# Transfers by index that name 128 rows instead of 96, in a mixture-of-experts kernel on one core

## The chip, the cores and the metric

The kernel runs on one core of one Trainium2 chip. The metric is the device time of one execution in microseconds (us). Before the change the median of three runs was 1855.05 us (1853.5 to 1856.7).

## What is computed

Two layers work on 512 latent tokens and 256 context tokens of width 1024. Each layer is a token mixer (retention and pooling) and then a mixture of 32 SwiGLU experts. The router gives each token two experts, and each expert computes on the tokens that it was given:

```python
def run_block(args):
    tok, e = args
    xb = h_pad[tok]
    return (jax.nn.silu(xb @ w_gate[e]) * (xb @ w_up[e])) @ w_down[e]
...
y_buf = y_buf.reshape(n_rows, D).astype(jnp.float32) * buf_w[:, None]
return jax.ops.segment_sum(y_buf, buf_tok, num_segments=T + 1)[:T].astype(h.dtype)
```

The first layer routes all 768 tokens, the second the 512 latent tokens alone. Weights are float32, and every expert has three matrices of 2 MiB each, so that each expert's weights are 6 MiB that are read once.

## The kernel before

The program is written out by hand for each engine, in order, with no scheduler; the names PE (TensorE), DVE (VectorE), ACT (ScalarE), POOL (GpSimd) and SP (the queue that issues the weight loads) are those of the profile.

Weights. `pump()` (L141) issues loads of 1 MiB each on SP into a ring of seven `raw` tiles; six loads make an expert. ACT (L1335) turns a `raw` tile into a float16 high part, DVE (L1340) makes the low part that is left, and the `raw` tile is then free for the next load. One of the six (the second half of the down matrix) is kept as float32 and is read by PE itself (L1283).

Tokens. Each expert has a capacity of CAP = 96 slots, numbered from 0 without holes; an expert with more tokens would go to `overflow_blocks` (L1347), which none does for these inputs. `rt.si[slot, e]` is the token's row, and for a slot without a token it is a number past the last row (8192 is added in L1106 and L1107). `fetch` (L1212) is a DMA by index: it reads the rows of 4 KB that the 96 slots of an expert name from `hs` in HBM into `xg`, slot by slot, and skips a row whose index is out of bounds. The slots with a token are called live below, the others dead. `turn` (L1219) transposes `xg` on PE, and `turned` (L1230) copies the result for the matmuls, the second half of it on ACT (L1234).

Results. `down_out` (L1286, ACT) writes the weighted result of an expert into a tile `ye` of 128 x 2 x 1024 float32, of which rows 0 to 95 are used; in the first layer `gate_rows` (L1289, POOL) fills the second half of that tile with the gate of each row. `scatter` (L1298) multiplies by the gate on POOL (L1303), and `scatter_rows` (L1306) is again a DMA by index: it adds the 96 rows of 4 KB to the rows of `xs` in HBM that the index names, and skips those out of bounds.

Order. In the loop over experts (L1539), expert e's down projection and scatter are followed by the transposition of expert e+2's rows and by the fetch for expert e+4, then by expert e+1's up projection. POOL therefore sees, per expert: gate rows, two multiplications, a scatter, a fetch. The tiles `whi`, `wlo`, `wd`, `ye`, `xg` and some others share a pool `G` of 14 buffers, and a new tile takes a free one.

Of the kernel before, what the change touches and what calls it, by code (L numbers as in the profile page):

```python
# [8 lines left out]
F32 = mybir.dt.float32  # L9
# [9 lines left out]
D = 1024  # L19
# [7 lines left out]
CAP = 96  # L27
# [14 lines left out]
def kernel(ctx: ExitStack, tc: tile.TileContext, a: dict, out: bass.AP):  # L42
# [10 lines left out]
    def G(shape, dt, name):  # L53
        return pg.tile(shape, dt, name=name, tag="G")
# [4 lines left out]
    def W(shape, dt, name="wt"):  # L59
        return pw.tile(shape, dt, name=name, tag="W")  # L60

    def S(shape, dt=F32, name="st"):
        return ps_.tile(shape, dt, name=name, tag="S")

    def P(shape, name="pt"):
        return pp.tile(shape, F32, name=name, tag="P")

    V, A, Q, T = nc.vector, nc.scalar, nc.gpsimd, nc.tensor
# [5 lines left out]
    hs = [pd.tile([(6 - 2 * l) * 128, 2 * D], F16, name=f"hs{l}") for l in range(DEPTH)]  # L74
# [98 lines left out]
    for j in range(2):  # L173
        t = G([128, 2, D], F32, "x")
# [856 lines left out]
    class Route:  # L1031


        def __init__(self, l, nt):
            self.nt = nt
            self.tmp = G([128, nt, 232], F32, "rtmp")
            self.L = self.tmp[:, :, 0:40]
            V.memset(self.L[:, :, 36:40], -1e30)
            self.ix = W([128, nt, 16], U32, "rix")
            self.oh = W([128, nt, 32], F16, "roh")  # L1040
            self.v4 = pc.tile([128, nt, 32, 4], F16, name=f"rv{l}", tag="rv")
            self.posm = pc.tile([128, nt, 32], F32, name=f"rp{l}", tag="rp")
            self.ov = pc.tile([128, 6, 32], F32, name=f"ov{l}", tag="ov")

            self.si = pc.tile([128, 32], I32, name=f"si{l}", tag="si")
            self.sv = pc.tile([128, 2, 32], F32, name=f"sv{l}", tag="sv")
            self.novi = pc.tile([1, 1], I32, name=f"nov{l}")

        def choose(self, i, between=()):
# [162 lines left out]
    def fetch(l, xg, si):  # L1212

        Q.indirect_dma_start(  # L1214
            out=xg[0:CAP], out_offset=None, in_=hs[l],
            in_offset=bass.IndirectOffsetOnAxis(ap=si, axis=0), bounds_check=(6 - 2 * l) * 128 - 1,
            oob_is_err=False)

    def turn(xg):  # L1219

        out = []
        for r in range(2):
            pt = pp.tile([128, KC, CAP], F16, name="pgx", tag="P")
            for c in range(KC):
                o = r * D + c * 128
                T.transpose(pt[:, c, :], xg[0:CAP, o:o + 128], ident16[0:CAP, 0:CAP])
            out.append(pt)
        return out

    def turned(pts):  # L1230
        xh = W([128, KC, CAP], F16, "xh")
        xl = W([128, KC, CAP], F16, "xl")
        V.tensor_copy(xh, pts[0])  # L1233
        A.copy(xl, pts[1])  # L1234
        return xh, xl

    def slot_vals(pe, v4e, nt):
        pv = P([128, 512], "psv")
        for i in range(nt):
            T.matmul(pv[0:CAP, 0:4], lhsT=pe[:, i, :], rhs=v4e(i), start=(i == 0), stop=(i == nt - 1))  # L1240
        sv = S([128, 8], F32, "sv")
        si = S([128, 1], I32, "si")
        V.tensor_copy(sv[0:CAP, 0:1], pv[0:CAP, 0:1])
        V.tensor_reduce(sv[0:CAP, 1:2], pv[0:CAP, 1:4], axis=AX.X, op=ALU.add)
        V.tensor_scalar(sv[0:CAP, 1:2], sv[0:CAP, 1:2], IWS / VS, None, op0=ALU.mult)
        V.tensor_scalar(sv[0:CAP, 2:3], sv[0:CAP, 0:1], 0.5, 8192.0, op0=ALU.is_lt, op1=ALU.mult)
        V.scalar_tensor_tensor(si[0:CAP], sv[0:CAP, 0:1], -1.0, sv[0:CAP, 2:3], op0=ALU.add, op1=ALU.add)
        V.tensor_scalar(sv[0:CAP, 3:4], sv[0:CAP, 0:1], NLAT + 0.5, None, op0=ALU.is_gt)
        return sv, si
# [39 lines left out]
    def gate_rows(yg, ctx, g2r, nv):  # L1289

        if nv == 1:
            return [g2r[0:CAP, 0, n * 512:(n + 1) * 512] for n in range(2)]
        gn = yg[0:CAP, 1, :]
        Q.tensor_scalar(gn, g2r[0:CAP, 1, :], ctx, None, op0=ALU.mult)  # L1294
        Q.tensor_tensor(gn, gn, g2r[0:CAP, 0, :], op=ALU.add)
        return [gn[:, n * 512:(n + 1) * 512] for n in range(2)]

    def scatter(l, yg, si, gs, eng):  # L1298

        yt = yg[:, 0, :]  # L1300
        for n in range(2):
            yn = yt[0:CAP, n * 512:(n + 1) * 512]
            eng.tensor_tensor(yn, yn, gs[n], op=ALU.mult)  # L1303
        scatter_rows(l, yg, si)

    def scatter_rows(l, yg, si):  # L1306
        Q.indirect_dma_start(  # L1307
            out=xs[l], out_offset=bass.IndirectOffsetOnAxis(ap=si, axis=0),
            in_=yg[0:CAP, 0, :], in_offset=None, bounds_check=6 * 128 - 1, oob_is_err=False,
            compute_op=ALU.add)  # L1310

    natives = {}
# [30 lines left out]
    def moe(l, h2, rt, pe0, nt, post_load=None):  # L1343
# [3 lines left out]
        def overflow_blocks():  # L1347

            _, vals = nc.values_load_multi_w_load_instructions(
                rt.novi[0:1, 0:1], engines=mybir.ALL_ENGINES, min_val=0, max_val=16)  # L1350
# [4 lines left out]
            with tc.If(nov > 0):  # L1355
                with tc.For_i(0, nov) as _i:
# [10 lines left out]
                    _, ev = nc.values_load_multi_w_load_instructions(  # L1367
                        eix[0:1, 0:1], engines=[ET.SP], min_val=0, max_val=NE - 1)
# [13 lines left out]
                    pe = W([128, nt, CAP], F16, "pe")  # L1382
                    make_sel(pe, pb, range(nt))
                    sv, si = slot_vals(pe, lambda i: vb[:, i, :], nt)
                    fetch(l, xg[:, 0], si[0:CAP, :1])
                    xe = turned(turn(xg[:, 0]))
                    rawb = R([128, 2048], F32, "raw")
                    wb = [G([128, 4096], F16, n) for n in ("whi", "wlo")]
# [22 lines left out]
                    yg = G([128, 2, D], F32, "ye")  # L1411
# [64 lines left out]
            return rt.sv[0:CAP, 0, e:e + 1]  # L1476

        def slot(e):
            return rt.si[0:CAP, e:e + 1]

        def rows_of(e):
            yg = G([128, 2, D], F32, "ye")
            return yg, gate_rows(yg, rt.sv[0:CAP, 1, e:e + 1], g2r, nv)

        xg = G([128, 2, 2 * D], F16, "xg")
        Q.memset(xg[0:CAP].bitcast(F32), 0.0)
        pe, g0 = pe0
        xe = gather_last(h2, pe, nt, g0)
        pgt = P([128, 4, CAP], "pgate")
# [2 lines left out]
        for e in (1, 2):  # L1492
            fetch(l, xg[:, e % 2], slot(e))
# [12 lines left out]
        rt.values()  # L1506
        hi_(1, 1, 1)
        yg, gs = rows_of(0)
        w, raw = convs.pop((l, 0, 2)), natives.pop((l, 0))
        xt_ = turn(xg[:, 1])  # L1510
        for n in range(2):
# [3 lines left out]
            down_out(pt, weight(0), yg[:, 0, :], n)  # L1515
        lo_()
        scatter(l, yg, slot(0), gs, Q)
        pgt = P([128, 4, CAP], "pgate")
        gate_up(convs.pop((l, 1, 0)), xe, pgt)
# [15 lines left out]
        for e in (3, 4):  # L1535
            fetch(l, xg[:, e % 2], slot(e))
        xe = xn
        pes = None
        for e in range(1, NE):  # L1539
# [6 lines left out]
            sgd = sg  # L1546
            w, raw = convs.pop((l, e, 2)), natives.pop((l, e))
            yg, gs = rows_of(e)
            if e == NE - 2:
                st["depth"] = NR - 2  # L1550
# [37 lines left out]
            if e == 8:  # L1588
                rt.overflow()
        overflow_blocks()  # L1590
        if l == 0:
            st["depth"] = 4
# [3 lines left out]
        if l == 0:  # L1596
            scatter_rows(l, yg, slot(NE - 1))
# [74 lines left out]
    mix, job = mixer(0, hT, True, pls)  # L1672
    h2, rt, pe0 = out_and_route(0, mix, job, 6)
    xt = moe(0, h2, rt, pe0, 6)
    xt.append(G([128, 2, D], F32, "x"))
    nc.sync.dma_start(out=xt[2], in_=xs[0][512:768, :].rearrange("(t p) d -> p t d", p=128))
# [13 lines left out]
    h2, rt, pe0 = out_and_route(1, mix, job, 4)  # L1690
    fg = []

    def load_fg():
        fg.append(G([128, D], F32, "fg"))
        nc.sync.dma_start(out=fg[0], in_=a["fng"].unsqueeze(0).to_broadcast([128, D]))

    xl = moe(1, h2, rt, pe0, 4, load_fg)
    late = None
    for i in range(5):
# [92 lines left out]
```

## Time and profile before

| what | value |
|---|---|
| median of the runs | 1855.05 us (1853.5 to 1856.7) |
| the profiled execution's own time | 1856.79 us |
| its span | 1855.0 us |
| mean granted clock of TensorE | 0.943 |
| busy share of PE, DVE, ACT, POOL | 87%, 72%, 55%, 56% |
| bytes moved by DMA | 542.31 MB, a mean of 292 GB/s |

The share of an engine is its busy time over the span. The profile's chain of work that ended last reaches back only to 1828.5 us, so it says nothing of the experts; what sets their pace has to be read from the stretches in which they run, from the first layer's first scatter at 406.7 us to its last at 984.5 us, and in the second layer from 1272.8 us to 1823.1 us.

### The profile page before, as it was taken

The page shows a single profiled execution, that of the slowest core. Times are in us where ns is not written, and L with a number is a line of the kernel's source. Part 1 is how long each engine was busy: PE and PEld are TensorE (multiplying, and loading weights), DVE is VectorE, ACT ScalarE, POOL GpSimd, SP SyncE. Part 2 cuts the span into 40 slices and gives each one's busy share as a digit, 9 for nine tenths or more (in the row PEclk, how much of TensorE's full clock was granted, in tenths as well). Part 3 has the DMA queues.
Part 4 walks back from the last instruction along what each step waited for, and adds up shares of the span by engine and source line. Part 5 has one row for each costly group of instructions (what it writes and reads, how often), then busy time and mean ns, then how long its engine had stood idle before and what let it go on. Part 6 is the DMA issues. An engine that isn't in the chain of part 4 may idle for free. (4 is left out here: it accounts for less than half of the span.)

```text
span 1855.0 us, 43386 instructions
## 1 busy us (share of the span) xinstructions
PE 1609.5 (87%) x19059; PEld 1179.5 (64%) x19059; DVE 1330.5 (72%) x1451; ACT 1020.3 (55%) x1040; POOL 1032.4 (56%) x526
## 2 busy tenths in 40 slices
PE   6999999868888888888878999887888888889885
PEld 3567775556666666666654677566676666667663
DVE  5665567878789767777776877787767776666764
ACT  4433342446665666666654444346666666666662
POOL 1222234547898889998894333252554555454553
PEclk9999999889999999999998999988999999989998
DMA  9644564579998999999983455667999999999993
GB/s 386 234 159 155 183 227 153 174 231 375 382 359 326 383 364 344 370 358 361 364 318 143 136 196 180 269 213 268 377 366 348 378 354 369 352 357 357 360 348 116
DMA packets 123293, 542.31 MB, mean 292 GB/s; under 512 B 17594, under 2 KB 18666, under 8 KB 87000
## 3 DMA queue, kind: packets, MB, share of 16 engines
q1 hardware_dynamic: 105384, 507.87, 73.0%
q0 software_dynamic: 14000, 20.54, 4.7%
q10 hardware_dynamic: 3712, 11.04, 1.5%
q8 instruction: 153, 2.51, 0.5%
q14 instruction: 44, 0.36, 0.1%
HBM read 530.59 MB, written 37.43 MB: 306 GB/s over the span
## 5 line engine op out<-in xcount | busy, mean ns | idle before, releaser
L1340 DVE SCALAR_TENSOR_TENSOR wlo<-raw,whi 128x2048 f16<-128x2048 f32 x248 | 589.3, 2410 | 216.5 <-ACT whi L1335 216.4
L1335 ACT ACTIVATE whi<-raw 128x2048 f16<-128x2048 f32 x248 | 472.8, 1910 | 316.8 <-DMA raw<-in_exp_w_up_dram 279.3
L420 PEld LDWEIGHTS <-wlo 128*128 128x128 f16 x4512 | 458.3, 102 | 175.6 <-issue 144.5
L418 PEld LDWEIGHTS <-whi 128*128 128x128 f16 x4512 | 459.1, 102 | 45.9 <-issue 16.6
L419 PEld LDWEIGHTS <-whi 128*128 128x128 f16 x4512 | 458.8, 102 | 40.4 <-issue 11.2
L419 PE MATMUL pgate<-xl,whi 128*128 128x96 f16 x2048 | 308.1, 220 | 132.8 <-ACT xl L1234 132.5
L418 PE MATMUL pgate<-xh,whi 128*128 128x96 f16 x2048 | 312.1, 220 | 5.0 <-DVE xh L1233 4.8
L1303 POOL TENSOR_TENSOR ye<-ye,modrow 96x512 f32<-96x512 f32 x62 | 163.0, 2628 | 264.4 <-ACT ye L1287 264.4
L420 PE MATMUL pgate<-xh,wlo 128*128 128x96 f16 x2048 | 308.1, 220 | 0.0
L418 PE MATMUL pup<-xh,whi 128*128 128x96 f16 x2048 | 266.3, 206 | 0.0
L420 PE MATMUL pup<-xh,wlo 128*128 128x96 f16 x2048 | 266.1, 206 | 0.0
L419 PE MATMUL pup<-xl,whi 128*128 128x96 f16 x2048 | 266.0, 206 | 0.0
L1283 PE MATMUL pdn<-raw,sg 128*96 128x512 f32 x512 | 243.9, 599 | 0.0
L1307 POOL DMA_INDIRECT xs<-ye,si x63 | 171.4, 2721 | 21.5 <-POOL ye L1303 17.3
L1340 DVE SCALAR_TENSOR_TENSOR wd<-raw,wd 128x2048 f16<-128x2048 f32 x64 | 163.2, 2549 | 16.5 <-ACT wd L1335 16.3
L1294 POOL TENSOR_SCALAR ye<-modrow,sv 96x1024 f32<-96x1024 f32 x32 | 162.3, 5073 | 1.4
L1303 POOL TENSOR_TENSOR ye<-ye 96x512 f32<-96x512 f32 x62 | 134.7, 2183 | 49.3 <-ACT ye L1287 47.3
L1283 PEld LDWEIGHTS pdn<-raw,sg 128*96 128x96 f32 x512 | 85.2, 166 | 89.7 <-issue 71.1
L1335 ACT ACTIVATE wd<-raw 128x2048 f16<-128x2048 f32 x64 | 122.2, 1910 | 21.1 <-DMA raw<-in_exp_w_down_dram 21.1
L418 PE MATMUL pdn<-wd,at 128*96 128x512 f16 x256 | 100.1, 391 | 20.8 <-ACT at L1271 11.1
L1214 POOL DMA_INDIRECT xg<-hs,si x62 | 94.3, 1521 | 36.8 <-issue 23.2
L405 DVE SCALAR_TENSOR_TENSOR wlo<-raw,whi 128x2048 f16<-128x2048 f32 (+1 forms) x36 | 82.8, 2305 | 40.2 <-ACT whi L404 40.2
(308 smaller groups left out, 3094.7 us busy)
## 6 DMA issues: line engine op xcount, KB each, us to landing
raw<-in_exp_w_gate_dram SPq DMA_DIRECT2D x128, 1024.0 KB
raw<-in_exp_w_up_dram SPq DMA_DIRECT2D x128, 1024.0 KB
raw<-in_exp_w_down_dram SPq DMA_DIRECT2D x128, 1024.0 KB
raw<-in_ada_w_dram SPq DMA_DIRECT2D x32, 1024.0 KB
raw<-in_w_in_dram SPq DMA_DIRECT2D x20, 1024.0 KB
raw<-in_ada_dram SPq DMA_DIRECT2D x16, 1024.0 KB
raw<-in_w_out_dram SPq DMA_DIRECT2D x8, 1024.0 KB
xs<-xr ACTq DMA_DIRECT2D x10, 512.0 KB
```

The lines of the kernel that those rows point to most:

```text
L405: V.scalar_tensor_tensor(lo, t, WS, hi, op0=ALU.mult, op1=ALU.subtract)
L418: T.matmul(o, lhsT=lh, rhs=rh, start=first, stop=False)
L419: T.matmul(o, lhsT=lh, rhs=rl, start=False, stop=False)
L420: T.matmul(o, lhsT=ll, rhs=rh, start=False, stop=last)
L1214: Q.indirect_dma_start(out=xg[0:CAP], out_offset=None, in_=hs[l], in_offset=bass.IndirectOffsetOnAxis(ap=si, axis=0), bounds_check=(6 - 2 ...
L1283: T.matmul(pt[0:CAP, :], lhsT=sg[:, f, :], rhs=raw[:, f - 2, sl], start=False, stop=(f == 3))
L1294: Q.tensor_scalar(gn, g2r[0:CAP, 1, :], ctx, None, op0=ALU.mult)
L1303: eng.tensor_tensor(yn, yn, gs[n], op=ALU.mult)
L1307: Q.indirect_dma_start(out=xs[l], out_offset=bass.IndirectOffsetOnAxis(ap=si, axis=0), in_=yg[0:CAP, 0, :], in_offset=None, bounds_check=6 ...
L1335: A.activation(hi[:, sl, :], t, AF.Copy, scale=WS)
L1340: V.scalar_tensor_tensor(lo, t, WS, hi, op0=ALU.mult, op1=ALU.subtract)
```

## The change

Both transfers by index name 128 rows. The index tables get the out-of-bounds number 8192 in rows 96 to 127, written once for each layer (and once for each overflow block), so the 32 further rows are always dead. `fetch` writes all of `xg`, which is zeroed over 128 rows instead of 96. `scatter_rows` takes as many rows as its index has: 128 in the expert loop, 96 still in the overflow block. Since the scatter now reads rows 96 to 127 of `ye`, that tile is no longer taken from the pool for each expert: two tiles `yes` are taken once for each layer, their rows 96 to 127 are set to zero on POOL, and expert e uses tile e % 2. The two tiles come out of the same 14 buffers.

```diff
             self.si = pc.tile([128, 32], I32, name=f"si{l}", tag="si")
             self.sv = pc.tile([128, 2, 32], F32, name=f"sv{l}", tag="sv")
+            V.memset(self.si[CAP:128], 8192)
...
     def fetch(l, xg, si):
         Q.indirect_dma_start(
-            out=xg[0:CAP], out_offset=None, in_=hs[l],
+            out=xg, out_offset=None, in_=hs[l],
...
         si = S([128, 1], I32, "si")
+        V.memset(si[CAP:128], 8192)
...
             out=xs[l], out_offset=bass.IndirectOffsetOnAxis(ap=si, axis=0),
-            in_=yg[0:CAP, 0, :], in_offset=None, bounds_check=6 * 128 - 1, oob_is_err=False,
+            in_=yg[0:si.shape[0], 0, :], in_offset=None, bounds_check=6 * 128 - 1, oob_is_err=False,
             compute_op=ALU.add)
...
-                    fetch(l, xg[:, 0], si[0:CAP, :1])
+                    fetch(l, xg[:, 0], si[:, :1])
...
         def slot(e):
-            return rt.si[0:CAP, e:e + 1]
+            return rt.si[:, e:e + 1]
+
+        yes = [G([128, 2, D], F32, "ye") for _ in range(2)]
+        for t in yes:
+            Q.memset(t[CAP:128, 0], 0.0)

         def rows_of(e):
-            yg = G([128, 2, D], F32, "ye")
+            yg = yes[e % 2]
             return yg, gate_rows(yg, rt.sv[0:CAP, 1, e:e + 1], g2r, nv)

         xg = G([128, 2, 2 * D], F16, "xg")
-        Q.memset(xg[0:CAP].bitcast(F32), 0.0)
+        Q.memset(xg.bitcast(F32), 0.0)
```

## Rows read from the trace of the kernel before

**Rows 1.** The page: busy PE, and the DMA engines in 40 slices.
```profile
PE 1609.5 (87%) x19059; PEld 1179.5 (64%) x19059; DVE 1330.5 (72%) x1451; ACT 1020.3 (55%) x1040; POOL 1032.4 (56%) x526
...
DMA  9644564579998999999983455667999999999993
```

**Rows 2.** Busy time in two stretches, one of each layer.
```profile
core 0: us, PE busy (x) PEld busy (x) DVE busy (x) ACT busy (x) POOL busy (x), PEclk, DMA share, GB/s
...
600.00:660.00 60.00, 52.18 (x760) 40.57 (x757) 46.13 (x33) 39.67 (x34) 53.13 (x21) 0.97 0.99 377
...
1500.00:1560.00 60.00, 51.21 (x752) 40.04 (x750) 41.92 (x30) 40.21 (x35) 32.22 (x14) 0.97 0.97 359
```

**Rows 3.** Waits from 420 to 1000 us: total us, times, longest.
```profile
ACT whi L1335 <- DMA raw<-in_exp_w_up_dram: 137.7, 44, 5.9
...
PE pgate L419 <- ACT xl L1234: 62.9, 25, 4.4
...
SPq L145 <- DVE wlo L1340: 235.7, 88, 11.1
```

**Rows 4.** DMA queues, 430 to 960 us: packets, bytes, share of sixteen engines.
```profile
q1 hardware_dynamic: 33322, 180.61, 89.0%
q0 software_dynamic: 6160, 10.55, 8.3%
```

**Rows 5.** DMA rate in 40 slices and queues, 1290 to 1800 us.
```profile
GB/s 413 384 378 360 369 372 362 364 349 349 378 315 398 379 380 343 360 388 329 357 389 342 350 373 351 348 360 370 356 339 354 357 362 386 359 333 370 378 330 352
...
q1 hardware_dynamic: 31437, 176.73, 91.1%
q0 software_dynamic: 6142, 7.07, 5.8%
```

**Rows 6.** The fetches (L1214) of both layers: count, durations, first and last start.
```profile
L1214 POOL DMA_INDIRECT xg<-hs,si x27: 1017/1422/2642, 436.5 to 921.3; - x27
...
L1214 POOL DMA_INDIRECT xg<-hs,si x27: 997/1426/2307, 1302.9 to 1779.7; - x27
```

**Rows 7.** One scatter alone, 1825.10 to 1825.42 us: its DMA packets.
```profile
DMA packets 64, 0.03 MB, mean 104 GB/s; under 512 B 56, under 2 KB 56, under 8 KB 64
```

**Rows 8.** The same scatter, 1825.42 to 1828.00 us.
```profile
DMA packets 50, 0.18 MB, mean 71 GB/s; under 512 B 9, under 2 KB 9, under 8 KB 48
...
q0 software_dynamic: 48, 0.16, 36.6%
```

**Rows 9.** The same scatter, its end alone, 1827.47 to 1827.80 us.
```profile
DMA packets 7, 0.00 MB, mean 0 GB/s; under 512 B 7, under 2 KB 7, under 8 KB 7
```

**Rows 10.** DMA queues, 570 to 690 us, where experts have few tokens.
```profile
q1 hardware_dynamic: 7318, 41.48, 90.6%
q0 software_dynamic: 1391, 1.37, 4.5%
```

**Rows 11.** DMA queues, 830 to 960 us, where experts have many tokens.
```profile
q1 hardware_dynamic: 8855, 43.46, 87.9%
q0 software_dynamic: 1431, 3.57, 11.4%
```

**Rows 12.** Indexed transfers' queue: 420 to 570, 1290 to 1450, 1450 to 1640 us.
```profile
q0 software_dynamic: 1746, 2.76, 8.0%
...
q0 software_dynamic: 1792, 2.64, 7.0%
...
q0 software_dynamic: 2445, 2.23, 5.1%
```

**Rows 13.** POOL's groups by line: busy us, mean ns, idle before.
```profile
L1307 POOL DMA_INDIRECT xs<-ye,si x63 | 171.4, 2721 | 21.5 <-POOL ye L1303 17.3 <-DVE xl L1459 4.0 <-DVE at L1272 0.3
...
L1214 POOL DMA_INDIRECT xg<-hs,si x62 | 94.3, 1521 | 36.8 <-issue 23.2 <-DMA hs<-h 9.1 <-PE pgate L420 4.6
```

**Rows 14.** POOL in order of time at the first layer's start of experts.
```profile
368.31 1.80 POOL L1486 MEMSET xg<- 96x2048 f32 x1
379.55 1.30 POOL L1214 DMA_INDIRECT xg<-hs,si  x1 [9.44 <-issue]
```

## The prediction

> **What bounds the kernel now.** I read the page first. PE is the busiest engine and the DMA engines are near their limit in two long stretches, the two loops over experts [rows 1]. In these stretches no compute engine is full: PE works 51 to 52 of 60 us, DVE 42 to 46, POOL 53 in the first layer and 32 in the second, while the sixteen DMA engines are busy 0.97 to 0.99 of the time [rows 2]. The waits say the same: ACT waits for weight loads, PE waits for ACT's copy of the transposed tokens, which stands behind those waits in ACT's order, and SP waits for a free `raw` tile, which only means that the ring of seven is full [rows 3]. So the DMA side sets the pace. An expert takes (921.3 - 436.5) / 26 = 18.65 us in the first layer and (1779.7 - 1302.9) / 26 = 18.34 us in the second, from the fetches' first and last start [rows 6].
>
> A busy share of 0.99 looks as if all sixteen engines were full, and then only the sum of bytes would count. The rows speak against that. A transfer by index makes 112 packets, 96 rows and 16 completions: 64 of the last scatter stand in one window and 48 in the next [rows 7, 8]. So packets over 112 are transfers, and bytes over 4096 are live rows. From 570 to 690 us this gives 1.37 MB / 4096 / (1391 / 112) = 27 live rows a transfer, from 830 to 960 us 68 [rows 10, 11]. The weight loads of an expert (6 x 1.049 MB) took 120 us / (41.48 / 6.29) = 18.2 us in the first stretch and 130 / (43.46 / 6.29) = 18.8 us in the second. 41 more rows in each of two transfers, at 0.27 us a row over sixteen engines, would be 1.4 us if the sum counted; 0.6 us is there. The pace hangs little on how many rows are live.
>
> What does set it is where the live rows go. In its first 0.32 us the lone scatter finishes 56 small packets and starts 8 large ones [rows 7]. 56 is eight engines times (6 dead rows + 1 completion): eight engines had nothing but dead rows. The other eight take 2.4 us more for the rest: 39 large packets by their 0.16 MB, 47 live rows in all [rows 8]. Seven completions then come together at the end [rows 9]: seven engines with six live rows each, and one with five. So rows go to engines in blocks of six, and since slots are filled from 0, the first engine carries six live rows in every transfer, however few tokens the expert has (six or more), and the last ones carry hardly any. Check this against the pace. The fastest slice moves 413 GB/s [rows 5], 25.8 GB/s an engine, so an engine's 64 KB of a load take 2.54 us and six loads 15.2 us. A live row costs 8.3% x 530 us x 16 / 2576 rows = 0.273 us in the first layer [rows 4] and 5.8% x 510 x 16 / 1726 = 0.274 us in the second [rows 5], dead rows and completions included. The first engine has 12 of them an expert: 3.3 us. The sum is 18.5 us, against 18.65 and 18.34 measured. An engine without live rows needs 15.2 us. The loop runs at the pace of the DMA engines that carry slots 0 to 5; the others' busy share must hold waiting.
>
> **The change, part by part.** 128 rows over sixteen engines are 8 each. If blocks stay blocks, the first engine carries eight live rows instead of six in each transfer (every stretch of rows 10 to 12 has a mean of 25 or more, so eight are live nearly always). Per expert that is 2 transfers x 2 rows x 0.273 = 1.09 us on the engine that sets the pace. The lower bound of a row is its bytes at the line rate, 4096 / 25.8 GB/s = 0.16 us for a fetch, and as much again for a scatter that reads before it adds, if it does so in turn: 0.24 us in the mean. The upper bound is 0.274. I take 0.273, since it was measured beside the same loads.
>
> How many transfers count? In the two bound stretches the packets give 6160 / 112 + 6142 / 112 = 110 [rows 4, 5], so 110 x 2 x 0.273 = 60 us if all of it passes; with all 125 transfers [rows 13] 68 us; with 0.24 us a row and seven tenths passing (there are slices of 315 and 329 GB/s in which something else held the loads [rows 5]) 37 us. I take 60 x 0.85 = 51 us.
>
> The 32 dead rows: in the lone scatter seven small packets pass on each of eight engines within 0.32 us, so at most 0.05 us each. Under blocks of eight they all lie on the last four engines, which have time. Cost 0.
>
> POOL: a scatter of 96 rows holds it 2.72 us and a fetch 1.52 us [rows 13]. If none of this grows with the rows it is 0, if all of it does it is a third, 1.4 us an expert. In the first layer POOL is busy 53.13 / 60 x 18.65 = 16.5 us an expert [rows 2], so at 17.9 us it would still fit. What it would make late is the next scatter and the fetch for four experts on, which is used two experts later. I take 0, since the longer period of the DMA side leaves POOL some 2 us; without that cover it is the fourth rival. In the second layer half of POOL is free.
>
> The memsets: `xg` over 96 rows and 2048 columns takes 1.80 us [rows 14]; two of 1024 columns are some 1.8 us more in each layer. Behind them POOL waits 9.44 us before its first fetch [rows 14], so 0; without that cover 3.6 us. The DVE memset of `si` is 32 columns at a place without a queue: 0.
>
> The fixed `ye` tiles: the gate rows and `down_out` of expert e wait for the scatter of e-2, one period and more before; a lone scatter is through in under 3 us [rows 7, 8], and beside the loads six or eight rows per engine alternate with load packets, under 10 us. Cost 0. The pool keeps 10 free buffers for five tiles an expert, where it had 12 for six: two experts' worth either way. ACT's waits name loads, not buffers [rows 3]. Cost 0, with 2 us at each layer's start as the upper bound.
>
> The last scatter takes a third longer, under 1 us, and lies beside the last matmuls.
>
> Sum: 1856.79 + 51 = 1908 us for the profiled execution, whose time is 1.7 us above the median, so 1906 us.
>
> **Rivals.** First, other blocks. 128 rows might be dealt in groups of four over eight engines, rows 32 to 63 going to the same eight again. The first engine then has 4 live rows where an expert has up to 32 tokens, 8 from 36 on. By the means of five stretches (43, 27 and 68 rows in the first layer, 40 and 25 in the second [rows 10 to 12]) 440 us lie above 36 and 310 below 32, about 35 and 25 experts: 35 x 1.09 = +38 us, and -27 us of which perhaps half passes before PE, at 52 of 60 us, is next. With 0.85 of the loss passing, as above, that is 32 - 13 = +19 us, 1874 us, between 1850 and 1890. For it speaks that eight rows an engine can be cut into groups of four, as six could not; against it, that 96 rows go in plain blocks. [...]
>
> Second, the sum counts after all: all sixteen engines full, where the live rows lie is indifferent, and only dead packets are added. 64 more an expert are 4 per engine, at most 4 x 0.05 us x 60 = 11 us, more likely 2: 1855 to 1860 us. For it speaks the share of 0.99 [rows 2], against it the steady pace at 27 and 68 rows.
>
> Third, the other side: a finer deal. If 128 rows were spread so that the first engine gets three rows or fewer live (single rows in turn: 47 rows over 16), it loses six rows an expert, 1.6 us, until PE is the bound: at half passing -50 us, 1805 us. It decides as soon as the first engine gets fewer than six. Against it: at 96 rows the deal is in blocks [rows 7 to 9].
>
> Fourth, POOL: if its transfers grow by all of the third and also wait on each other, the first layer's 16.5 us become 18 and more and the loop follows POOL: some 0.5 us x 30 = +15 us, 1870 us. It decides above 18.6 us.
>
> **How the numbers follow.** Blocks of eight 0.52, own range 1892 to 1923 (37 and 68 us added); groups of four 0.24, of which 0.16 slower, 0.04 within and 0.04 faster; the sum 0.14, of which 0.12 within and 0.02 slower; a finer deal 0.05; POOL 0.05. A measurement of this kernel can tell about 0.2%, 3.7 us. Faster 0.09, same 0.16, slower 0.75. The likeliest case gives 1906 us. For eight in ten the range reaches over the groups of four and most of the second rival, down to 1857, and up to 1923.
>
> **What would show it.** In the profile after: transfers of 144 packets; in the lone last scatter more engines done at once (at 47 live rows ten, then 10 x 9 = 90 small packets) and a longer tail; periods of 19.3 to 19.7 us; loads still near 15.2 us on a free engine, q0 and q1 together down from 361 GB/s (191.16 MB in 530 us [rows 4]) to about 342; longer waits of ACT for loads. If the early small packets stay those of eight engines and completions come in two batches, the groups of four are right. If the period stays within 0.1 us, the engine that I name was not the bound. The prediction fails by its central step if the deal of rows changes with their number.

## The result, and the profile after

The changed kernel takes 1833.45 us (1828.98 to 1835.06), against 1855.38 us for the kernel before: a ratio of 0.988 (95% interval 0.986 to 0.990). It is 22 us faster, where 51 us slower was forecast. Run once more it came to 0.988 (0.985 to 0.992). Its profiled execution took 1832.03 us, with a span of 1830.3 us.

The page of the changed kernel, busy times and DMA engines in 40 slices, beside [rows 1]:

```profile
PE 1610.0 (88%) x19059; PEld 1178.2 (64%) x19059; DVE 1346.8 (74%) x1453; ACT 1020.0 (56%) x1040; POOL 1030.3 (56%) x530
...
DMA  9635455569998999999994354747999999999993
```

PE, ACT and POOL have the work that they had; in the loops over experts the DMA engines are still busy for 1.00 of the time from 600 to 660 us and 0.99 from 1500 to 1560 us, beside 0.99 and 0.97 [rows 2]. The waits of ACT, PE and SP from 420 to 1000 us (total us, times, longest), beside [rows 3]:

```profile
ACT whi L1337 <- DMA raw<-in_exp_w_up_dram: 123.9, 45, 6.1
...
PE pgate L419 <- ACT xl L1235: 55.3, 25, 4.9
...
SPq L145 <- DVE wlo L1342: 239.1, 84, 8.8
```

ACT waits 14 us less for loads and PE 8 us less for ACT. The fetches of the two layers (count, durations, first and last start), beside [rows 6]:

```profile
L1215 POOL DMA_INDIRECT xg<-hs,si x27: 1084/1348/2539, 436.6 to 918.1; - x27
...
L1215 POOL DMA_INDIRECT xg<-hs,si x27: 1057/1352/2432, 1295.9 to 1754.8; - x27
```

The period is 481.5 / 26 = 18.52 us in the first layer (18.65 before) and 458.9 / 26 = 17.65 us in the second (18.34 before). The gain is in the second layer, where experts have fewer tokens. Now the deal of the rows. The last scatter, alone on the DMA engines: all packets and its queue from 1801.40 to 1805.00 us, and the packets of three windows in it (1801.40 to 1801.90, 1802.90 to 1803.35 and 1803.35 to 1805.00 us):

```profile
DMA packets 146, 0.22 MB, mean 60 GB/s; under 512 B 97, under 2 KB 97, under 8 KB 144
...
q0 software_dynamic: 144, 0.19, 37.5%
...
DMA packets 70, 0.05 MB, mean 99 GB/s; under 512 B 61, under 2 KB 61, under 8 KB 69
...
DMA packets 26, 0.02 MB, mean 55 GB/s; under 512 B 20, under 2 KB 20, under 8 KB 26
...
DMA packets 24, 0.07 MB, mean 45 GB/s; under 512 B 7, under 2 KB 7, under 8 KB 23
```

It has 144 packets, 128 rows and 16 completions. Of these 97 are small, so 47 are live rows, as many as in the last scatter before. In blocks of eight, ten of sixteen engines would have been done at once, with 90 small packets; there are 61, and eight engines with nothing but dead rows can have 8 x (8 + 1) = 72. Then, more than a microsecond later and well before the end, 20 small packets pass within 0.45 us: four engines with four dead rows and a completion each. These four had four live rows and then dead ones, while others still move live rows until 1805 us. That is the deal of the first rival, and the sign that the prediction had named for it: groups of four rows over eight engines, the second half of 64 rows on the same eight again. The trace names no engine of a packet, but the sums agree: 61 + 9 of the 72 pass before 1802.90 us, and the 7 of the last window can be the other two with one dead row and four completions of the engines that go on. 72 + 20 + 5 makes the 97, and 4 x 4 + 3 x 8 + 7 the 47 live rows. The packets of the 96 rows had fitted blocks of six [rows 7 to 9].

Queues from 430 to 960 us and from 1290 to 1740 us (packets, MB, share of sixteen engines), the first beside [rows 4]:

```profile
q1 hardware_dynamic: 33820, 181.83, 88.2%
q0 software_dynamic: 8029, 10.72, 8.2%
...
q1 hardware_dynamic: 28914, 162.11, 92.4%
```

The share times the time over the megabytes is the time for which a megabyte of weights keeps the sixteen engines busy: 0.882 x 530 / 181.83 = 2.571 us, where the kernel before has 2.612 [rows 4]. The packets of the weight loads, which the change does not touch, have become shorter. This was in no step of the prediction.

### The profile page after: what moved, and what is told of

It reads as the page before. It is cut to its first block, busy times and chain, and to the rows that moved or that the text cites. A ratio compares the mean times of both kernels' runs of the same rounds, so it can differ in the third digit from the quotient of the medians.

```text
span 1830.3 us, 43421 instructions
## 1 busy us (share of the span) xinstructions
PE 1610.0 (88%) x19059; PEld 1178.2 (64%) x19059; DVE 1346.8 (74%) x1453; ACT 1020.0 (56%) x1040; POOL 1030.3 (56%) x530
## 3 DMA queue, kind: packets, MB, share of 16 engines
q8 instruction: 153, 2.51, 0.5%
## 5 line engine op out<-in xcount | busy, mean ns | idle before, releaser
L1342 DVE SCALAR_TENSOR_TENSOR wlo<-raw,whi 128x2048 f16<-128x2048 f32 x248 | 599.1, 2447 | 187.6 <-ACT whi L1337 187.3
L1309 POOL DMA_INDIRECT xs<-ye,si x63 | 183.3, 2910 | 22.5 <-POOL ye L1305 17.5
L1296 POOL TENSOR_SCALAR ye<-modrow,sv 96x1024 f32<-96x1024 f32 x32 | 145.2, 4538 | 1.3
L418 PE MATMUL pdn<-wd,at 128*96 128x512 f16 x256 | 100.1, 391 | 16.4 <-ACT at L1273 8.6
```

The lines of the kernel that those rows point to most:

```text
L418: T.matmul(o, lhsT=lh, rhs=rh, start=first, stop=False)
L1309: Q.indirect_dma_start(out=xs[l], out_offset=bass.IndirectOffsetOnAxis(ap=si, axis=0), in_=yg[0:si.shape[0], 0, :], in_offset=None, bounds ...
L1342: V.scalar_tensor_tensor(lo, t, WS, hi, op0=ALU.mult, op1=ALU.subtract)
```

## The experiments

Every run is set against the kernel before on the same chip. The period is (last - first start) / (count - 1) of the fetches, as above; it is that of one profiled execution, while the ratio is of medians. The changed kernel's two profiles give 18.52 and 18.53 us in the first layer and 17.65 and 17.73 in the second. But the fixed tiles alone have shorter periods than the kernel before although that execution took 1863.01 us, 6 us longer, and the profiled execution of blocks of six (1829.42 us) is the fastest of its six, 11 us under their median. So differences of 0.1 to 0.2 us in a period say little.

| run | rows named: fetch, scatter | most live rows on one engine | ratio (95% interval) | median us | period, layer 1 and 2, us |
|---|---|---|---|---|---|
| before | 96, 96 | 6 | 1 | 1855 | 18.65, 18.34 |
| change | 128, 128 | 4 up to 32 tokens, 8 from 36 | 0.988 (0.986 to 0.990) | 1833.45 | 18.52, 17.65 |
| fixed tiles alone | 96, 96 | 6 | 1.003 (1.001 to 1.005) | 1858.42 | 18.53, 18.18 |
| fetch alone | 128, 96 | 4 or 8; 6 | 0.994 (0.991 to 0.997) | 1842.48 | 18.32, 18.05 |
| scatter alone | 96, 128 | 6; 4 or 8 | 1.004 (1.002 to 1.005) | 1860.36 | 18.79, 18.25 |
| blocks of eight | 128, 128 | 8 | 1.021 (1.019 to 1.024) | 1889.45 | 19.10, 19.04 |
| blocks of six | 128, 128 | 6 (7 or 8 above 80 tokens) | 0.992 (0.990 to 0.995) | 1840.56 | 18.07, 18.03 |
| blocks of six, scatter at 96 | 128, 96 | 6 | 0.990 (0.986 to 0.994) | 1840.45 | 18.16, 18.20 |
| blocks of six, fetch at 96 | 96, 128 | 6 | 0.997 (0.996 to 0.999) | 1852.99 | 18.66, 18.28 |
| 96 rows, dealt | 96, 96 | n / 16, rounded up | 0.966 (0.962 to 0.971) | 1789.13 | 17.74, 16.66 |
| 128 rows, dealt | 128, 128 | n / 16, rounded up, to n = 64 | 0.958 (0.955 to 0.961) | 1773.47 | 17.62, 16.24 |
| before, fetch all dead | 96, 96 | 0; 6 | 0.965 (0.961 to 0.969) | 1788.94 | 17.50, 17.01 |

**First set: theory A, the deal of the rows, against B, the fixed tiles, and C, cheaper rows.** The renumbered runs change one table only, which slot takes which token; transfers, indices and all instructions of the loops stay.

Fixed tiles alone, in the kernel before:

```diff
+        yes = [G([128, 2, D], F32, "ye") for _ in range(2)]
         def rows_of(e):
-            yg = G([128, 2, D], F32, "ye")
+            yg = yes[e % 2]
```

> The kernel before with only the two fixed result tiles: both transfers still name 96 rows. Theory A (the gain of the change comes from how 128 rows are dealt to the DMA engines): nothing, 1851 to 1859 us. Rival B (the tiles that no longer rotate free the pool and remove a wait): most of the 22 us that the change gained, 1833 to 1840 us.

Measured: 1.003. B falls; the tiles gain nothing, and cost some 5 us.

Fetch alone: as the change, with `ye` from the pool and the scatter's rows and index cut to 96.

> The kernel before with the fetch alone naming 128 rows; the scatter names 96 and its tiles rotate. Theory A: a fetched row costs its engine about half of a scattered one (0.16 against 0.33 us by the bounds in the prediction), so about a third of the gain, 7 us: 1845 to 1851 us. Rival B: nothing, 1855 us.

Measured: 0.994, 11 us, more than a third of the gain. B falls again, and A's share of the fetch is too small.

Blocks of eight, in the changed kernel:

```diff
-    V.tensor_scalar(iot1, iot[:, 0:CAP], 1.0, None, op0=ALU.add)
+    cols(iot1[:, 0:64].rearrange("q (a c d) -> q a c d", a=2, d=4),
+         iot[:, 0:64].rearrange("q (c a d) -> q a c d", a=2, d=4))
+    cols(iot1[:, 64:96], iot[:, 64:96])
```

(`cols` is the same addition of 1.)

> The changed kernel with the slots renumbered so that the first engine gets the first eight tokens, the second the next eight, and so on up to 64: the layout that the prediction had assumed. Theory A, with the prediction's price for a row: 37 to 68 us above the kernel before, 1892 to 1923 us. Rival B and a rival C (with 128 rows each row is cheaper, wherever it lies): it stays at 1833 us, or at least below 1855 us.

Measured: 1889 us, 1.021, slower than both kernels by a mere renumbering. Where live rows lie does set the pace; but the loss is at the lower end of the range, by the median 3 us below it.

The 96 rows dealt, in the kernel before:

```diff
-    V.tensor_scalar(iot1, iot[:, 0:CAP], 1.0, None, op0=ALU.add)
+    V.tensor_scalar(iot1.rearrange("q (g o) -> q g o", o=6), iot[:, 0:CAP].rearrange("q (o g) -> q g o", g=16),
+                    1.0, None, op0=ALU.add)
```

> The kernel before, 96 rows and rotating tiles, with the slots renumbered so that the tokens are dealt one by one over the sixteen engines (slot 6g + o takes token 16o + g). An engine then has at most 3 live rows at a mean of 46 tokens and 2 at 30, in place of 6. Theory A: 3 to 4 rows less in each of two transfers, 1.6 to 2.2 us an expert until another engine is the bound: 1755 to 1815 us. Rivals B and C: nothing, 1855 us.

Measured: 1789 us, 0.966, some three times the gain of the change, without the change. A holds.

**Second set: is the deal all?** The next kernel puts the first eight engines back to six live rows each, with 128 rows named.

```diff
+    six = iot[:, 0:48].rearrange("q (c k) -> q c k", k=6)
+    far = iot1[:, 32:64].rearrange("q (c d) -> q c d", d=4)
+    cols(iot1[:, 0:32].rearrange("q (c d) -> q c d", d=4), six[:, :, 0:4])
+    cols(far[:, :, 0:2], six[:, :, 4:6])
...
```

> The changed kernel with the slots renumbered so that each of the first eight engines gets six tokens in a row, as in the kernel before; from the 49th token on the others get four. Theory A alone: all of the gain is undone, 1850 to 1858 us. Theory A with rival C: a row costs 0.24 instead of 0.27 us (from the run with blocks of eight, which lost 36 us where 0.273 us a row gave 61), so 12 rows save 0.4 us an expert and 1828 to 1838 us is left.

Measured: 0.992. A alone fails: at six live rows an engine, as before, 14 us of the gain are still there. With C it misses by 3 us (1840.56). The fetches of blocks of six, and then of blocks of eight:

```profile
L1215 POOL DMA_INDIRECT xg<-hs,si x27: 1082/1349/2485, 434.6 to 904.3; - x27
...
L1215 POOL DMA_INDIRECT xg<-hs,si x27: 1056/1354/2433, 1284.9 to 1753.8; - x27
```

```profile
L1215 POOL DMA_INDIRECT xg<-hs,si x27: 1082/1345/2472, 435.2 to 931.7; - x27
...
L1215 POOL DMA_INDIRECT xg<-hs,si x26: 1057/1599/2433, 1305.8 to 1781.9; - x26
```

Between these two only the numbering differs, with two live rows more per transfer on the fullest engines, and the period goes from 18.07 to 19.10 and from 18.03 to 19.04 us: 1.0 us an expert, for 1.09 in the prediction (2 x 2 x 0.273). The price of a row was about right. Nor is a row much cheaper under 128: the queue of the indexed transfers gives 8.2% x 530 us x 16 / 2617 rows = 0.266 us in the changed kernel, by the line above, and 0.273 before.

> The changed kernel with the fetch back at 96 rows, the scatter at 128 with its fixed tiles. The fetch alone gained 11 us. If the two parts add up, the other 11 us and the 5 us that the fixed tiles cost: 1838 to 1846 us. If the gain needs both on the same layout, 1850 us or more.

Measured: 1.004, 1860 us. The sum fails, and the time is that of the second case; but the third set shows that the gain at equal blocks does not need both. The scatter alone gains nothing. Its periods move as the deal would have it, up in the first layer (18.79) and down in the second (18.25), but shifts of 0.14 and 0.09 us are too small to tell.

> The changed kernel (128 rows, groups of four) with the slots renumbered so that up to 64 tokens are dealt over all sixteen engines, at most ceil(n / 16) live rows each, as in the run that dealt 96 rows. Theory A alone (only the largest number of live rows on one engine counts): the same as that run, 0.960 to 0.972 of the kernel before, 1780 to 1800 us. Theory A with rival C (a row also costs less under the layout of 128): 3 to 8 us below that run.

Measured: 0.958, 16 us below the run that dealt 96 rows, in the direction of C and twice as far.

**Third set: fetch or scatter?** Blocks of six again, with one transfer back at 96 rows, so the number of live rows on the fullest engine is six in all of them.

```diff
-            out=xs[l], out_offset=bass.IndirectOffsetOnAxis(ap=si, axis=0),
-            in_=yg[0:si.shape[0], 0, :], in_offset=None, bounds_check=6 * 128 - 1, oob_is_err=False,
+            out=xs[l], out_offset=bass.IndirectOffsetOnAxis(ap=si[0:CAP], axis=0),
+            in_=yg[0:CAP, 0, :], in_offset=None, bounds_check=6 * 128 - 1, oob_is_err=False,
...
```

> The run with blocks of six at 128 rows, with the scatter back at 96 rows (its fullest engine has six live rows with this numbering too). Theory D (what is left of the gain at equal blocks comes from the fetch, whose writes under the layout of 96 rows make the weight loads' packets longer): the whole of it stays, 0.990 to 0.996 of the kernel before, loop period 17.7 to 17.9 us in both layers. Rival E (it comes from the scatter, or needs both on one layout): 1.000 to 1.005, period 18.2 to 18.3 us.

```diff
-            out=xg, out_offset=None, in_=hs[l],
-            in_offset=bass.IndirectOffsetOnAxis(ap=si, axis=0), bounds_check=(6 - 2 * l) * 128 - 1,
+            out=xg[0:CAP], out_offset=None, in_=hs[l],
+            in_offset=bass.IndirectOffsetOnAxis(ap=si[0:CAP], axis=0), bounds_check=(6 - 2 * l) * 128 - 1,
...
```

> The run with blocks of six at 128 rows, with the fetch back at 96 rows and the scatter at 128. Theory D: nothing is left but the price of the fixed tiles, 1.000 to 1.006 of the kernel before, period 18.2 to 18.3 us. Rival E: 0.990 to 0.996, 17.7 to 17.9 us.

Measured: 0.990 with the fetch at 128 and the scatter at 96, and 0.997 the other way round, a little below D's bound. The ratios go with D; the period of the first layer does too (18.16 against 18.66), that of the second does not tell (18.20 against 18.28). The periods that D had given for the fetch at 128, 17.7 to 17.9 us, are missed by 0.3 us.

> The kernel before with every row of every fetch out of bounds, so the experts after the first compute on zeros and no fetched row moves; all instructions stay. It prices the fetch at 96 rows. By the prediction's 0.273 us, or 0.16 by the bytes, six rows on the first engine are 1.0 to 1.6 us an expert: 1758 to 1795 us. Theory D: the loads' packets also get shorter, to the 2.55 to 2.57 us per MB over all engines that runs with the fetch at 128 rows show, from 2.61. Rival: the packets' length stays at 2.61 us per MB, and something else made it shorter there.

```diff
-                    fetch(l, xg[:, e % 2], slot(e + 4))
+                    fetch(l, xg[:, e % 2], none[0:CAP])
...
```

(`none` holds 8192 in every row; the fetches before the loop take it too.)

Measured: 1789 us, within the price. The weight loads' queue from 430 to 900 and from 1290 to 1740 us in four kernels (packets, MB, share): before; blocks of six with the fetch at 96; blocks of six with the scatter at 96; no live fetch.

```profile
q1 hardware_dynamic: 28547, 160.13, 89.0%
...
q1 hardware_dynamic: 27887, 156.64, 91.2%
```

```profile
q1 hardware_dynamic: 28507, 159.90, 89.7%
...
q1 hardware_dynamic: 27915, 156.71, 91.6%
```

```profile
q1 hardware_dynamic: 29275, 164.64, 89.5%
...
q1 hardware_dynamic: 28082, 157.74, 90.8%
```

```profile
q1 hardware_dynamic: 30445, 171.26, 92.7%
...
q1 hardware_dynamic: 29774, 166.69, 94.3%
```

Per megabyte: 2.61 and 2.62 us before; 2.64 and 2.63 with the fetch at 96; 2.55 and 2.59 with the fetch at 128; 2.54 and 2.55 with no fetched row. So in blocks of six the load packets are 1 to 3% longer with the fetch at 96 than with the fetch at 128, and with that up to 2% longer than with no fetched row. An expert's 6.29 MB save 0.36 and 0.19 us, against 0.49 and 0.14 us of period (18.65 and 18.34 to 18.16 and 18.20).

But this mean also moves with the deal. The same lines of blocks of eight, of 96 rows dealt and of 128 rows dealt give 2.60 and 2.63, 2.55 and 2.50, 2.50 and 2.43 us:

```profile
q1 hardware_dynamic: 27913, 156.66, 86.8%
...
q1 hardware_dynamic: 26912, 151.08, 88.2%
```

```profile
q1 hardware_dynamic: 30026, 168.31, 91.2%
...
q1 hardware_dynamic: 30537, 170.76, 94.7%
```

```profile
q1 hardware_dynamic: 30290, 170.20, 90.4%
...
q1 hardware_dynamic: 30120, 168.39, 91.1%
```

With 96 rows dealt the packets are as short as with no fetched row at all, so the mean alone cannot say what the layout does. The single packets of the traces can: those of the weight loads, from 430 to 900 and from 1290 to 1690 us, are split by whether their middle falls between the first and the last 4 KB row of indexed transfers (rows less than 1 us apart) or in the rest of the time. In us per MB, first and second layer:

| run | fetch | beside indexed rows | in the rest of the time |
|---|---|---|---|
| before | 96 | 2.73, 2.73 | 2.56, 2.57 |
| blocks of six, fetch at 96 | 96 | 2.74, 2.72 | 2.58, 2.58 |
| 96 rows, dealt | 96 | 2.67, 2.63 | 2.51, 2.47 |
| blocks of six, scatter at 96 | 128 | 2.52, 2.62 | 2.57, 2.56 |
| blocks of six | 128 | 2.49, 2.54 | 2.58, 2.59 |
| 128 rows, dealt | 128 | 2.42, 2.42 | 2.52, 2.44 |
| before, fetch all dead | 96, none live | 2.57, 2.52 | 2.54, 2.54 |

Beside indexed rows the load packets are 6 to 7% longer with live rows fetched into 96 rows, also when dealt (5 to 8% with the two runs left out here, fixed tiles alone and scatter alone); with the fetch at 128, or with no live row fetched, they are between 4% shorter and 3% longer, the runs left out here included. In the kernel before that is 2.61 us per MB in all against 2.56 in the rest of the time: 0.05 x 6.29 = 0.3 us an expert, an estimate of 17 us over 54 experts, beside the 14 us of the gain that are there at equal blocks. Why the rest of the time differs between the deals (2.44 to 2.59) is not shown.

> The changed kernel once more, on the chip of the other three. All theories: 0.986 to 0.990 of the kernel before, loop periods near 18.2 us in the first layer and 17.7 us in the second.

Measured: 0.988, periods 18.53 and 17.73 us. The expectation for the first layer is missed; the first run of the changed kernel had 18.52.

## Why the prediction was wrong

**What bounds the kernel: right.** The engines that carry the first slots set the pace. Three renumberings that change nothing else move the time by -62 us (0.966 of 1855), +54 us (from blocks of six, 0.992, to eight, 1.021) and -56 us (from the change, 0.988, to the dealt rows, 0.958). That its check of the pace came out at 18.5 us was partly luck: it took the loads at the rate of the fastest slice, 15.2 us an expert, but by [rows 4] their packets took 0.89 x 530 / 180.61 x 6.29 = 16.4 us in the mean, which with 3.3 us of rows is 19.7, above the measured period. Such a sum need not be the time of an engine, and how far they overlap on the fullest one is not known.

**The failing step: "If blocks stay blocks, the first engine carries eight live rows instead of six in each transfer."** They don't stay blocks: by the 61, 20 and 7 small packets of the last scatter 128 rows go in groups of four, so the first engine has four live rows with up to 32 tokens and eight only from 36 on. The prediction took the deal from 96 rows and carried it to 128, though its own first rival named another deal. The price hung on that step was sound: 51 us for two rows more, and 54 measured from blocks of six to blocks of eight made by hand (some 40 against the kernel before, which has the longer packets).

**The first rival named the deal and still had the sign wrong**, +19 us. Its groups of four over eight engines were an assumption that no trace of the kernel before shows; the last scatter of 128 rows does. Its counts were right. In the run with no live fetch every live row is a scatter's, and the trace counts 9 experts with up to 32 tokens and 23 with 36 or more in the first layer, and 18 and 13 in the second, whose last expert is not scattered; the rival had 25 and 35 in all. Two things were mis-sized. It let half of a gain pass before PE would be the bound. By these counts the dealt rows leave the fullest engine 2.5 rows less than blocks of six in the first layer and 3.5 in the second, in each of two transfers, 1.4 and 1.9 us an expert by price; the periods fell by 0.45 and 1.79 us (18.07 to 17.62 and 18.03 to 16.24). So a third passes in the first layer and nine tenths in the second, which has 18 of the 27 experts with few tokens. And it left out the weight loads' packets: 14 us of the 22 are there at equal blocks of six. What remains, from blocks of six to the change, is small and not well measured: 7 us faster by the medians, with intervals of 0.990 to 0.995 and 0.986 to 0.990, and 3 us slower by the profiled executions, with 0.45 us more in the first layer and 0.38 less in the second.

**Why the packets get shorter is not shown.** Shown is that it goes with the fetch's layout and not with the scatter's (in blocks of six 2.55 and 2.59 us per MB with the fetch alone at 128, 2.64 and 2.63 with the scatter alone), and that it is there while indexed rows pass (2.52 and 2.62 against 2.74 and 2.72 us per MB, and 2.57 and 2.56 against 2.58 and 2.58 in the rest of the time); of the two it is the fetch that writes tiles (`xg`), as the loads do (`raw`). The run with 96 rows dealt changed which rows are live, not which engine writes which rows; a fetch of 96 rows in groups of four was not tried.

**The costs put at nothing: right but for the fixed tiles.** These cost 0.3% alone (0.1 to 0.5), some 5 us, where the prediction had 0 and at most 2 us at each layer's start. POOL's transfers, the dead rows included, hardly grew, beside [rows 13]; the memsets lie in the wait before the first fetch, which starts at 379.35 us (379.55 before [rows 14]). POOL's groups after (busy us, mean ns, idle before):

```profile
L1309 POOL DMA_INDIRECT xs<-ye,si x63 | 183.3, 2910 | 22.5 <-POOL ye L1305 17.5 <-DVE xl L1461 5.0
L1215 POOL DMA_INDIRECT xg<-hs,si x62 | 91.6, 1477 | 32.5 <-issue 20.3 <-DVE wlo L1342 7.0 <-PE pgate L420 4.3
L1485 POOL MEMSET ye<- 32x1024 f32 x4 | 3.7, 958 | 0.1
```

A third more rows made the scatter 7% longer and the fetch 3% shorter.

**Open.** The fetch alone (-0.6%) and the scatter alone (+0.4%) don't add up to the change (-1.2%). In the first layer their periods do within what a period can tell (-0.33 and +0.14, against -0.13), in the second 0.3 us an expert is left over (-0.29 and -0.09, against -0.69). And the fixed tiles cost 0.3% alone, but the run with the fetch at 96 and the same tiles is 0.3% faster than before; where that lies was not found.

## What to carry to other kernels

Where transfers by index name more rows than are live, ask which DMA engine gets which row. Here the pace of a loop that streams weights was that of the engine with the most live rows, not of the sum, and a renumbering that adds no work to the loops dealt the rows evenly (a gain of 4.2% with 128 rows, 3.4% with 96). Don't carry a layout from one row count to another; find it in a lone transfer, from how many small packets pass at once and when the completions come. A mean busy share of 0.99 over sixteen engines [rows 2] did not say here that all were full: a renumbering of 96 rows took 3.4% off. And a mean length of packets says little before it is split by what passes beside them.

## What the runs showed of the hardware

The packets of the last scatter, with 47 live rows in both kernels, fit blocks of six on sixteen engines for 96 rows (56 small packets at once [rows 7], seven completions at the end [rows 9]) and, for 128 rows, groups of four with rows 0 to 63 on eight engines (61 small packets at once, 20 more in 0.45 us over a microsecond later). Renumberings made by that reading moved the time by -62, +54 and -56 us. A live row costs its engine 0.25 to 0.27 us in the mean of fetch and scatter beside a weight stream (1.0 us for four rows), while an out-of-bounds row is one of the small packets, of which an engine passes seven within 0.32 us [rows 7]. While live rows are fetched into 96 rows, the packets of unrelated weight loads are 5 to 8% longer than in the rest of the time, in five runs with different deals and scatters; with the fetch at 128 rows, or with no live row fetched, the two differ by at most 4%. Why is open.
